# One block of a hybrid decoder: z by seven products of 256 columns, step widths as a block of their own, down's weight sums by a table

## The chip, the cores and the metric

The program runs on one core of a Trainium2 chip. The metric is the time of one execution on the device in microseconds; the kernel before has a median of 1806.73 us over three runs (1806.51 to 1807.75). A profile is one execution of the same program, recorded by the hardware: its own time was 1806.8 us and the recorded span 1804.9 us. The core has a matrix engine (TensorE, PE in the profile, its weight loads PEld), a vector engine (VectorE, DVE), a scalar engine (ScalarE, ACT), GpSimd (POOL) and SyncE (SP), which here issues nearly all transfers.

## What is computed

One layer on 1024 tokens of 1024 channels, in float32. Cut to what matters here:

```python
h = rms_norm(x, pre_norm1_w) * (1 + sc1) + sh1
z, xbc, dt_raw, q, k, v, gates = split(h @ w_in)   # z: 1024 columns, dt_raw: 16
# state-space branch, 16 heads in chunks of 128 tokens
xbc = silu(causal_conv(xbc) + conv_b)
dt = softplus(dt_raw + dt_bias)
a_cum = cumsum(dt * -exp(a_log))       # over the tokens of a chunk, per head
y = ssd_chunked(...)                   # decays exp(a_cum[t] - a_cum[s])
y = (y + d_skip * xs) * silu(z)
y = rms_norm_by_group(y, eps=1e-5) * ssd_norm_w
# attention branch from q, k, v; both branches are merged by sigmoid(gates)
x = x + g1 * rms_norm(mix, post_norm1_w)
h2 = rms_norm(x, pre_norm2_w) * (1 + sc2) + sh2
u = causal_conv(h2 @ w_up)
f = (gelu(u_gate) * u_val) @ w_down
x = x + g2 * rms_norm(f, post_norm2_w)
```

A product of float32 matrices is made of three matrix products on TensorE: each factor is split into a high part (rounded to the matrix engine's format) and a low part (the rest), and high × high, high × low and low × high are added up. The function `split` does that for weights: the high part is a copy on ScalarE (L95), the low part a subtraction on VectorE (L96).

## The kernel before, in words

The order of instructions on TensorE, VectorE, ScalarE and SyncE is the order in which the code is written: these parts stand in a manual schedule, and a few generators and tables say at which point of a stage a side task takes its next step. Each engine goes through its own row in order and waits where an instruction's input or buffer is not ready.

**Opening** (to 94.83 us). h is made and transposed; the first projections and the gates' blocks 0 to 3 are computed as 24 matmuls of 512 columns for each half of the tokens. While the last gate blocks run, VectorE and ScalarE form sums and differences of the four quarters of h (first or second half of the channels, first or second half of the tokens): the left factors `t1` to `t4`. `gate_split` (L270) splits a gate block's weights, `gate_half` (L515) issues its matmuls, `gate_out` (L350) puts the result through an activation and stores it.

**Pairs** (94.83 to 380.75 us). Fifteen pairs of 256 columns each (q, k, xbc and gates). In place of eight products of quarter blocks, seven products of sums are made; `order` lists them with the quarter or sum of h that each uses (`b11`, `b21`, `t2`, `t1`, `t3`, `b22`, `t4` for the weights; `HX` for h) and the bank of PSUM into which it adds. `x_sum` (L400) forms the weight sums on VectorE, `x_split` their high and low parts, `post` (L456) evacuates a pair while the next one runs (for the convolution: three steps on VectorE per block, L499). In the last five pairs a side task runs: `all_sums` (L547) forms, for the last matrix of the layer (down), four sums of weight blocks for each of 11 k, 44 in all, and stores them for later. Two sets of tiles `wdr` are used in turn; 16 sums are made before z.

**z** (380.75 to 473.57 us). z and the 16 columns of dt_raw are one product of 1040 columns, in three thirds of 346, 346 and 348: for each third and each of eight blocks of 128 tokens `mm3` (L117 to L119) issues 24 matmuls, with h as the stationary factor. Each result goes through tanh on ScalarE (L970) and one step on VectorE (L971) and is stored; the first 16 columns of the first third become dt (L966). Beside it run the remaining 28 sums for down, the last pair's evacuation, the weights of the next third, and the decays: `decays_a` (L852 to L883: softplus of dt by a series of small steps, then `la` = dt × −exp(a_log)), `decays_b` (cumulative sums by two small matmuls, L887) and `decays_c` (transposes of them, L900, copied and stored for the chunks).

**v and the chunks** (from 473.57 us). v's matmuls (`v_stream`, L1042 to L1053) run with the chunks of the state-space branch between them (`chunk_in`, `chunk_decay`, ...). For v, weights are split by `split_v` (L912).

## Time and profile before

| | |
|---|---|
| median of three runs | 1806.73 us (1806.51 to 1807.75) |
| the profiled execution, its span | 1806.8 us, 1804.9 us |
| granted clock of TensorE, mean | 0.998 |
| busy share of the span: TensorE, VectorE, ScalarE, GpSimd | 99%, 76%, 51%, 6% |
| end of the opening, pairs, z | 94.83, 380.75, 473.57 us |
| z: TensorE, VectorE, ScalarE busy | 92.82, 56.35, 25.89 of 92.82 us |

A row of the stage table gives the stretch, its length, then busy us and the number of instructions of PE, PEld, DVE, ACT and POOL, then the granted clock, the share of the transfer engines and GB/s. In a row of single instructions the first number is the start, the second the duration; what stands in square brackets is the idle time of the engine just ahead of it and what ended it. In a row of a group stand the shape, the count, busy us, the mean duration in ns, and the idle time ahead of the group's instructions with what ended most of it. TensorE's matmuls overlap, so the distance from start to start is what one costs.

### The profile page before, as it was taken

The numbers are of one execution on the slowest core, as the hardware profiler recorded it, in microseconds if no ns is written. First come the engines' busy times: TensorE is split into PE (matmuls) and PEld (weight loads), VectorE is DVE, ScalarE is ACT, GpSimd is POOL, SyncE is SP. The second block draws the span as 40 slices with busy tenths as digits, with TensorE's granted clock in tenths as the row PEclk, the third lists the DMA queues.
The fourth block names the chain that finished last, engine by engine and source line by source line (L and its number), as shares of the span: only waits on it lengthen the run. The fifth ranks groups of instructions, "written<-read, shape, count | busy, mean of one in ns | idle before, by whom it ended". The sixth has DMA issues, their size and how long they took to land.

```text
span 1804.9 us, 24533 instructions
## 1 busy us (share of the span) xinstructions
PE 1782.1 (99%) x8749; PEld 1494.7 (83%) x8749; DVE 1364.5 (76%) x2245; ACT 919.6 (51%) x1794; POOL 111.7 (6%) x110
## 2 busy tenths in 40 slices
PE   8999999999999999999999999999999999999998
PEld 6788888899977888888888888888888888888887
DVE  6896788976488777666667876689898888875555
ACT  4454444543457556665555443665554554554532
POOL 0000000000155400000000000100000000000001
PEclk9999999999999999999999999999999999999999
DMA  9565687678878886679842576413232223378754
GB/s 358 190 213 172 240 273 257 189 243 274 272 255 243 253 254 172 178 205 278 260 145 100 181 254 253 152 53 117 99 129 99 100 100 111 123 244 288 239 164 165
DMA packets 165322, 356.18 MB, mean 197 GB/s; under 512 B 16064, under 2 KB 64976, under 8 KB 165200
## 3 DMA queue, kind: packets, MB, share of 16 engines
q1 hardware_dynamic: 165200, 354.62, 60.2%
q8 instruction: 69, 1.13, 0.3%
q14 instruction: 53, 0.43, 0.1%
HBM read 248.83 MB, written 103.62 MB: 195 GB/s over the span
## 4 chain that ended last, share of the span: by engine, by line
PE 55%; DVE 6%; DMA 5%; ACT 3%; issue 1%; SPq 1%; POOL 0%; DVEq 0%; POOLq 0%; ACTq 0%
PE upx L2025 4%; PE upx L2026 4%; PE upx L2024 4%; PE o L1531 2%; PE upy L2025 2%; PE upy L2024 2%; PE upy L2026 2%; PE dx L2416 2%; PE dx L2417 2%; PE dx L2415 2%; PE mix L2085 1%; PE mix L2087 1%; PE mix L2086 1%; PE at L1518 1%; DMA gst<-gld_a 1%
## 5 line engine op out<-in xcount | busy, mean ns | idle before, releaser
L2024 PE MATMUL upx<-t,wu_t 128*128 128x512 f32 x264 | 103.1, 391 | 0.5 <-DVE cv L2480 0.4
L2025 PE MATMUL upx<-t,wu_t 128*128 128x512 f32 x264 | 102.8, 390 | 0.2 <-DVE t L2142 0.2
L2026 PE MATMUL upx<-t,wu_t 128*128 128x512 f32 x264 | 102.8, 389 | 0.0
L1456 DVE CUSTOM_DVE_ANT_0 sc<-sc,mw 128x256 f32<-128x256 f32 (+7 forms) x128 | 96.2, 772 | 8.5 <-PE sc L1469 7.2
L1998 ACT ACTIVATE wu_t<-sab 128x512 fp32r<-128x512 f32 x57 | 34.1, 627 | 127.7 <-DVE sab L2015 127.7
L1519 ACT COPY aT<-at 128x512 f32<-128x512 f32 (+2 forms) x96 | 46.0, 479 | 95.7 <-PE at L1518 95.4
L96 DVE TENSOR_TENSOR g_lo<-gst,g_hi 128x1024 fp32r<-128x1024 f32 (+1 forms) x42 | 47.4, 1135 | 49.5 <-ACT g_hi L95 49.5
L1531 PEld LDWEIGHTS o<-vt,aT 128*128 128x128 f32 x576 | 76.0, 191 | 6.0 <-ACT aT L1519 0.7
L1531 PE MATMUL o<-vt,aT 128*128 128x128 f32 x576 | 79.9, 275 | 0.2 <-ACT aT L1519 0.2
L397 ACT ACTIVATE xw_t<-xsab 128x512 fp32r<-128x512 f32 x45 | 27.3, 627 | 94.6 <-DVE xsab L406 94.6
L95 ACT ACTIVATE g_hi<-gst 128x1024 fp32r<-128x1024 f32 (+1 forms) x42 | 41.3, 988 | 65.3 <-DMA gst<-gld_s 39.1
L422 PE MATMUL xx<-xt,xw_t 128*128 128x512 f32 x180 | 70.2, 390 | 0.0
L423 PE MATMUL xx<-xt,xw_t 128*128 128x512 f32 x180 | 70.1, 389 | 0.0
L424 PE MATMUL xx<-xt,xw_t 128*128 128x512 f32 x180 | 70.0, 389 | 0.0
L1468 PE MATMUL sc<-kst,qst 128*128 128x512 f32 (+2 forms) x192 | 66.0, 352 | 0.0
L1506 DVE RECIPROCAL rsm<-ssum 128x2 f32<-128x2 f32 x64 | 10.6, 166 | 72.9 <-ACT p L1497 39.7
L1469 PE MATMUL sc<-klo,qst 128*128 128x512 f32 (+2 forms) x192 | 63.3, 346 | 0.3 <-DMA klo<-kld 0.3
L2042 DVE SCALAR_TENSOR_TENSOR ug<-cg,vec,ug 128x1023 f32<-128x1023 f32 (+1 forms) x44 | 56.3, 1280 | 6.1 <-ACT ug L2041 5.3
L2002 DVE TENSOR_TENSOR wu_t<-sab,wu_t 128x512 fp32r<-128x512 f32 x57 | 39.3, 690 | 26.6 <-ACT wu_t L1998 26.6
L2024 PEld LDWEIGHTS upx<-t,wu_t 128*128 128x128 f32 x264 | 49.5, 188 | 11.8 <-DVE cv L2480 1.4
L2025 PEld LDWEIGHTS upx<-t,wu_t 128*128 128x128 f32 x264 | 49.6, 188 | 10.7 <-DVE t L2142 0.5
L1510 DVE SCALAR_TENSOR_TENSOR p<-p,coef,p 128x512 f32<-128x512 f32 (+2 forms) x96 | 56.6, 617 | 2.3
(580 smaller groups left out, 5804.1 us busy)
## 6 DMA issues: line engine op xcount, KB each, us to landing
adas<-in_w_ada SPq DMA_DIRECT2D x32, 512.0 KB, 6.2
wdr<-in_w_down SPq DMA_DIRECT2D x22, 512.0 KB, 5.2
wtd<-wdr SPq DMA_DIRECT2D x22, 512.0 KB, 3.4
wuf<-in_w_up SPq DMA_DIRECT2D x22, 512.0 KB, 3.5
gld_s<-gsum SPq DMA_DIRECT2D x22, 512.0 KB, 2.8
gst<-gld_s SPq DMA_DIRECT2D x20, 512.0 KB, 5.1
wdt_raw<-wtd SPq DMA_DIRECT2D x20, 512.0 KB, 4.4
wuv<-in_w_up SPq DMA_DIRECT2D x19, 512.0 KB, 3.5
```

The source lines that it names most:

```text
L422: T.matmul(o, wh, xh_, start=(k == 0 and first), stop=False, skip_group_check=not first)
L423: T.matmul(o, wh, xl_, start=False, stop=False, skip_group_check=not first)
L424: T.matmul(o, wl, xh_, start=False, stop=(k == KH - 1), skip_group_check=not first)
L1456: V.tensor_tensor_reduce(out=sc, in0=sc, in1=mw[:, S - L :], scale=1.0, scalar=3.0e38, op0=ALU.add, op1=ALU.min, accum_out=col)
L1468: T.matmul(sc[:, n0:n1], qs_[s][:, tsl], ks_[s][:, n0:n1], start=True, stop=False)
L1469: T.matmul(sc[:, n0:n1], qs_[s][:, tsl], kl[s][:, n0:n1], start=False, stop=True)
L1510: V.scalar_tensor_tensor(pr[0][:, ksl], pr[1][:, ksl], coef[:, bq : bq + 1], pr[0][:, ksl], op0=ALU.mult, op1=ALU.add)
L1531: T.matmul(po_of[j, grp][:, qi, :], at[:, k, :], vt[j % 2][:, kt, :], start=(kt == 0), stop=(kt == i))
L2024: T.matmul(out_, wh, xh_, start=(k == 0 and first), stop=False, skip_group_check=not first)
L2025: T.matmul(out_, wh, xl_, start=False, stop=False, skip_group_check=not first)
L2026: T.matmul(out_, wl, xh_, start=False, stop=(k == end), skip_group_check=not first)
L2042: V.scalar_tensor_tensor(u[:, d:], c_[:, : S - d], fw[:, 2 - d : 3 - d], u[:, d:], op0=ALU.mult, op1=ALU.add)
```

## The change

z becomes a product of the same kind as the pairs. Its 1024 columns are two halves of 512; a column group g takes 256 columns of each half, and for each of two groups seven products are made of four blocks of 128 tokens and 12 matmuls of 256 columns each. `z_sum` makes weight sums on VectorE, `z_split` high and low parts, `z_mms` the matmuls, `z_keep` copies a result out of PSUM on ScalarE, `z_out` adds a kept one on VectorE and applies Silu on ScalarE, then stores. The tiles `t1` to `t4` of h live through z, and one quarter of h is loaded again at z's end. The factor one half that came with tanh goes (`nwr` is no longer scaled, the norm's divisor changes).

The 16 columns of dt_raw become a block in the opening: `wdt` is a tile of 128 columns per k, of which 16 hold the high and 16 the low parts and the rest zero (set by GpSimd). 32 matmuls of 512 columns use it as the stationary factor, two copies on ScalarE bring the result to `dtacc`, and eight small matmuls with `sel` turn it and add the parts; VectorE adds dt_bias.

The sums for down are placed by a table (`down_at`: s is a sum, l a load); one set of tiles is used in pairs 2 to 5 and from pair 9, and a second one in z. The decays' steps are placed by `run_decays`. The accumulated sums and their transposes use other PSUM banks. The loads of the first decays and of z's rows are issued elsewhere.

```diff
+    def z_sum(i, g):
+        a11, a12, a21, a22 = (zleft[n, g] for n in ("a11", "a12", "a21", "a22"))
+        o, x_, y_, op = ((a21, a21, a22, ALU.add), (a11, a21, a11, ALU.subtract), (a21, a22, a11, ALU.subtract), (a12, a12, a11, ALU.subtract))[i]
+        V.tensor_tensor(o, x_, y_, op=op)
+
+    def z_split(i):
+        g, p = divmod(i, 7)
+        n = order[p][0]
+        hi = wp.tile([P, KH, ZW], F32R, tag="whi", name=f"wz{g}{n}_hi", bufs=4)
+        lo = wp.tile([P, KH, ZW], F32R, tag="wlo", name=f"wz{g}{n}_lo", bufs=4)
+        split(hi, lo, zleft[("a11", "a12", "a11", "a21", "a21", "a12", "a22")[p], g])
+        zop[i] = hi, lo
...
-    def down_sums(k):
-        (b11, b12), (b21, b22) = [(t[:, 0, :], t[:, 1, :]) for t in wdr[k % 2]]
-        V.tensor_tensor(b11, b12, b11, op=ALU.subtract)
-        yield
...
+    def down_sum(k, i):
+        (b11, b12), (b21, b22) = [(t[:, 0, :], t[:, 1, :]) for t in wset(k)]
+        o, x_, y_ = ((b11, b12, b11), (b12, b22, b12), (b22, b22, b11), (b21, b21, b22))[i]
+        V.tensor_tensor(o, x_, y_, op=ALU.subtract)
+        if i % 2 == 1:
+            SP.dma_start(wtd[i // 2][:, k, :, :], wset(k)[i // 2])
...
+    down_at = {(2, 4): "l", (2, 5): "l", (3, 3): "s", (3, 5): "s", (4, 0): "s", (4, 1): "ls", (4, 3): "l", (4, 5): "s", (4, 6): "s", (5, 2): "s", (5, 4): "s"}
...
+        wdt = wp.tile([P, KD, P], F32R, tag="whi", name="wdt", bufs=4)
+        G.memset(wdt.bitcast(F32), 0.0)
+        SP.dma_start(wdt_raw.rearrange("p k c -> p (k c)"), a["w_dt"])
...
+        split(wdt[:, :, :NH], wdt[:, :, NH : 2 * NH], wdt_raw)
+        V.reduce_sum(sel, ident.rearrange("p (j n) -> p n j", n=NH), axis=AX.X)
...
         pg_ = gate_half(2, 1)
+        pdt = [ps_wb("dt0"), ps_wc("dt1")]
+        for half in range(2):
+            for k in range(KD):
+                for n in range(2):
+                    T.matmul(pdt[half], wdt[:, k, :], hT[k][half][:, n, :], start=(k + n == 0), stop=(k == KD - 1 and n == 1))
         gate_out(pg, 0, gsd[2], vev)
+        dtacc = wp.tile([P, 2, HALF], F32, tag="wlo", name="dtacc", bufs=4)
+        for half in range(2):
+            A.copy(dtacc[:, half, :], pdt[half])
         gate_split(3)
         x_load()
...
+        pd = ps_wb("dt")
+        for i in range(8):
+            T.matmul(pd[:, i * NH : (i + 1) * NH], dtacc[:, i // 4, i % 4 * P : (i % 4 + 1) * P], sel, start=True, stop=True)
+        V.tensor_tensor(dtr, pd[:, :P].rearrange("p (c h) -> p c h", h=NH), rows[:, None, R_DTB : R_DTB + NH].broadcast_to([P, 8, NH]), op=ALU.add)
...
-        pa = ps_wa("acum_ps")
+        pa = ps_wc("acum_ps")
...
-            pt = ps_wa(f"acT_ps{half}")
+            pt = (ps_wb, ps_wc)[half](f"acT_ps{half}")
...
+    def z_mms(g, p, qs=range(4)):
+        n, bk = order[p]
+        bk = "X" if bk == "X" else "Y"
+        first = p in (0, 1, 3)
+        if first:
+            z_banks(g, bk, p, qs)
+        wh, wl = zop[7 * g + p]
+        for q in qs:
+            o = zbank[g, bk, q]
+            tsl = slice(q * P, (q + 1) * P)
+            for k in range(KH):
+                xh_, xl_ = HX[n][k][:, 0, tsl], HX[n][k][:, 1, tsl]
+                T.matmul(o, xh_, wh[:, k, :], start=(k == 0 and first), stop=False, skip_group_check=not first)
+                T.matmul(o, xh_, wl[:, k, :], start=False, stop=False, skip_group_check=not first)
+                T.matmul(o, xl_, wh[:, k, :], start=False, stop=(k == KH - 1), skip_group_check=not first)
+
+    def z_keep(g, bk, e, qs=range(4)):
+        for q in qs:
+            A.copy(zev[e][:, q, :], zbank[g, bk, q])
+
+    def z_out(g, h, half, bk, e, o):
+        t = zout[o]
+        for q in range(4):
+            if e is None:
+                A.activation(t[:, q, :], zbank[g, bk, q], AF.Silu)
+            else:
+                V.tensor_tensor(t[:, q, :], zbank[g, bk, q], zev[e][:, q, :], op=ALU.add)
+        if e is not None:
+            A.activation(t, t, AF.Silu)
+        z0 = HALF * h + ZW * g
+        SP.dma_start(zdh[half][:, :, z0 : z0 + ZW], t)
...
-                mm3(ps, [((hT[k][half][:, 0, tsl], hT[k][half][:, 1, tsl]), (wz[k // 2][0][:, k % 2, :], wz[k // 2][1][:, k % 2, :])) for k in range(KD)])
...
-                A.activation(e[:, 0, :n], ps[:, lo:], AF.Tanh, scale=0.5)
-                V.scalar_tensor_tensor(e[:, 1, :n], e[:, 0, :n], 1.0, ps[:, lo:], op0=ALU.add, op1=ALU.mult)
-                SP.dma_start(zd[i][:, c0 + lo - NH : c0 + lo - NH + n], e[:, 1, :n])
...
+        z_mms(0, 0)
+        z_sum(1, 0)
+        z_split(2)
+        z_split(3)
+        z_keep(0, "X", 0)
+        posts(0)
+        z_mms(0, 1)
...
+        z_mms(0, 4)
+        z_out(0, 1, 1, "X", 0, 1)
+        z_split(7)
+        wdr.append([SL.get(f"wdr1{j}", F32, (P, 2, HALF)) for j in range(2)])
+        down("ssll")
+        run_decays(5)
...
+        z_mms(1, 1)
+        z_out(1, 0, 0, "Y", 0, 0)
+        run_decays(5)
+        z_sum(2, 1)
+        z_split(11)
+        v_raw.append(fetch_v(0, 1))
+        down("ll")
+        z_mms(1, 2)
+        z_keep(1, "X", 1)
+        assert next(dec, None) is None
+        decays_b()
+        z_split(12)
+        SL.put(*HX["t2"])
+        down("ss")
+        v_raw.append(fetch_v(0, 2))
+        z_mms(1, 3, (0, 1))
+        decays_c()
+        z_mms(1, 4, (0, 1))
+        z_keep(1, "Y", 0, (0, 1))
+        z_mms(1, 3, (2, 3))
+        z_keep(1, "Y", 0, (2, 3))
+        z_split(13)
+        v_raw.append(fetch_v(0, 3))
+        SL.put(*HX["t1"])
+        xch = [SL.get(f"xch{i}", F32, (P, KD, P)) for i in range(2)]
+        zown = [SL.get(f"zown{n}", F32R, (P, 2, HALF)) for n in range(2)]
+        M = [SL.get(f"M{n}", F32, (P, NH // 2, P)) for n in range(3)]
+        SP.dma_start(xch[0], xcd[:, 0])
+        down("ss")
+        z_mms(1, 4, (2, 3))
+        z_out(1, 1, 1, "X", 0, 1)
+        split_v(0, 0, v_raw.pop(0), zown)
+        down("ssll")
+        SL.put(*HX["t3"])
+        for n in range(3):
+            load_decay(n)
+        SP.dma_start(xch[1], xcd[:, 1])
+        z_mms(1, 5)
+        z_out(1, 0, 1, "Y", 1, 0)
+        split_v(0, 1, v_raw.pop(0))
+        split_v(0, 2, v_raw.pop(0))
+        down("ss")
+        new_b12((0, 1))
+        z_mms(1, 6)
+        z_out(1, 1, 0, "X", None, 1)
+        split_v(0, 3, v_raw.pop(0))
+        down("ssss")
+        new_b12((2, 3))
...
-            lambda: rstd_of(ssy[:, c, :], ssy[:, c, :], 1.0 / (4 * GW), 1e-5),
+            lambda: rstd_of(ssy[:, c, :], ssy[:, c, :], 1.0 / GW, 1e-5),
```

Three places of the instruction rows. First, ScalarE in the opening. `gs_0` and `gs_1` are results of gate blocks, `vev` their tiles, `wgs_hi` the high part of gate block 3's weights, `xt` parts of `t1` and `t3`, `dt` the block's result in PSUM. Before:

```order
L352 ACTIVATE vev_696<-gs_1_418 128x512 [waits PE_49]
L521 ACTIVATE xt_0_739<-hr_123 128x512
L521 ACTIVATE xt_1_740<-hr_123 128x512
L352 ACTIVATE vev<-gs_0_700 128x512 [waits DMAHW4_49,PE_49,Activation_49]
L95 ACTIVATE wgs_hi<-wgs_raw 128x1024 [waits DMAHW6_49]
L521 ACTIVATE xt_2_741<-hr_124 128x512
```

There the high part of the weights follows the gate block's activation. In the change:

```order
L352 ACTIVATE vev_695<-gs_1_414 128x512 [waits PE_49]
L95 ACTIVATE wdt<-wdt_raw 128x8x16 [waits DMAHW1_49,Pool_49]
L528 ACTIVATE xt_0_738<-hr_123 128x512
L528 ACTIVATE xt_1_739<-hr_123 128x512
L352 ACTIVATE vev<-gs_0_699 128x512 [waits DMAHW4_49,PE_49,Activation_49]
L735 COPY dtacc<-dt_778 128x512 [waits PE_49]
L735 COPY dtacc<-dt_779 128x512 [waits PE_49]
L95 ACTIVATE wgs_hi<-wgs_raw 128x1024 [waits DMAHW6_49]
```

Two copies of the new block's results and the high part of its weights stand ahead of `wgs_hi`; both copies wait for TensorE.

Second, VectorE around the decays' last steps (`sm1` holds the decays' small tiles, `la` and `acum` among them, `acum_ps` and `acT_ps` are PSUM tiles of the cumulative sums and of their transposes, `wdr` the tiles of down's sums). Before, with z's rows of the third matmul group between them:

```order
L882 SCALAR_TENSOR_TENSOR sm1_3039<-sm1_3039,aexp_3044 128x128 [waits DVE_49,Activation_49]
L535 TENSOR_TENSOR wdr10_2395<-wdr11_2396,wdr10_2395 128x512 [waits DMAHW7_49]
L971 SCALAR_TENSOR_TENSOR ev0_3041<-ev0_3041,z346_4_3496 128x346 [waits DMAHW4_49,Activation_49]
L540 TENSOR_TENSOR wdr11_2396<-wdr11_2396,wdr10_2395 128x512 [waits DMAHW3_49,DVE_49]
L542 TENSOR_TENSOR wdr11_2396<-wdr11_2396 128x512 [waits DVE_49]
L96 TENSOR_TENSOR wz692_0_lo_3554<-wz692_0_raw_3400,wz692_0_hi_3553 128x696 [waits DMAHW0_49,Activation_49]
L971 SCALAR_TENSOR_TENSOR ev1_3042<-ev1_3042,z346_5_3528 128x346 [waits DMAHW7_49,Activation_49]
L533 TENSOR_TENSOR wdr00_2274<-wdr00_2274 128x512 [waits DMAHW6_49,DMAHW1_49]
L971 SCALAR_TENSOR_TENSOR ev2_3043<-ev2_3043,z346_6_3561 128x346 [waits DMAHW2_49,Activation_49]
L889 COPY sm1_3039<-acum_ps_3589 128x128 [waits PE_49]
L892 TENSOR_TENSOR sm1_3039<-acum_ps_3589,sm1_3039 128x128 [waits DVE_49,Activation_49]
```

The copy of the cumulative sums (L889) comes eight rows behind `la` (L882). In the change, from the step that makes `la` (L907) on:

```order
L907 SCALAR_TENSOR_TENSOR sm1_3096<-sm1_3096,aexp_3098 128x128 [waits DVE_49]
L368 TENSOR_TENSOR wza211_3305<-zxr_3033,wza111_3303 128x1024
L96 TENSOR_TENSOR wz1t3_lo_3712<-wza211_3305,wz1t3_hi_3711 128x1024 [waits Activation_49]
L914 COPY sm1_3096<-acum_ps_3771 128x128 [waits PE_49]
L917 TENSOR_TENSOR sm1_3096<-acum_ps_3771,sm1_3096 128x128 [waits DVE_49,Activation_49]
L96 TENSOR_TENSOR wz1b22_lo_3780<-wza121_3367,wz1b22_hi_3779 128x1024 [waits Activation_49]
L543 TENSOR_TENSOR wdr00_2341<-wdr00_2341 128x512 [waits DMAHW4_49,DMAHW2_49]
L543 TENSOR_TENSOR wdr00_2341<-wdr01_2342,wdr00_2341 128x512 [waits DMAHW3_49,DVE_49]
L926 COPY acs_3814<-acT_ps0_3815 16x512 [waits PE_49]
L926 COPY acs_3814<-acT_ps1_3821 16x512 [waits PE_49]
```

A weight sum and a low part of z now stand between `la` and the copy of the cumulative sums, and a low part and two sums for down between that copy and the copies of the transposes.

Third, TensorE at the same place, in the change (`z10`, `z13` are PSUM tiles of z's second column group):

```order
L995 MATMUL z10_3_3582<-wz1t2_hi_3567,xt2_3_642 128x256
L912 MATMUL acum_ps_3771<-sm1_3096,tri_148 128x128 [waits DMAHW6_49,DVE_49]
L913 MATMUL acum_ps_3771<-sm1_3096,ones_87 128x128
L993 MATMUL z13_0_3788<-wz1t1_hi_3635,xt1_0_738 128x256 [waits Activation_49]
L994 MATMUL z13_0_3788<-wz1t1_lo_3636,xt1_0_738 128x256
...
L995 MATMUL z13_1_3789<-wz1t1_hi_3635,xt1_3_741 128x256
L925 MATMUL acT_ps0_3815<-ident_83,sm1_3096 16x128 [waits DVE_49]
L925 MATMUL acT_ps0_3815<-ident_83,sm1_3096 16x128 x3
L925 MATMUL acT_ps1_3821<-ident_83,sm1_3096 16x128 [waits DVE_49]
L925 MATMUL acT_ps1_3821<-ident_83,sm1_3096 16x128 x3
L993 MATMUL z10_0_3579<-wz1t3_hi_3711,xt3_0_742 128x256 [waits Activation_49]
```

The cumulative sums stand between product (1, 2) and product (1, 3), the transposes after the first half of (1, 3).

254 lines of the change are left out of this document (121 added, 133 removed).

## The prediction

> **What bounds the kernel now.** I first read the busy times of the whole span, then the table of busy time by stage, cut at the places where the program's stages change, and then single instructions at the cuts.
>
> ```profile
> PE 1782.1 (99%) x8749; PEld 1494.7 (83%) x8749; DVE 1364.5 (76%) x2245; ACT 919.6 (51%) x1794; POOL 111.7 (6%) x110
> ...
> core 0: us, PE busy (x) PEld busy (x) DVE busy (x) ACT busy (x) POOL busy (x), PEclk, DMA share, GB/s
> ...
> 73.00:94.83 21.83, 21.83 (x98) 18.02 (x96) 17.10 (x28) 14.26 (x26) 0.00 (x0) 1.00 0.33 114
> 94.83:380.75 285.92, 285.92 (x1262) 236.31 (x1260) 240.27 (x343) 134.03 (x209) 0.00 (x0) 1.00 0.68 227
> 380.75:473.57 92.82, 92.82 (x590) 92.44 (x589) 56.35 (x108) 25.89 (x46) 0.00 (x0) 1.00 0.84 281
> ```
>
> ```profile
> 94.60 0.39 PE L119 MATMUL gs<-hT,wgs_lo 128*128 128x512 f32 x1
> 94.83 0.39 PE L422 MATMUL xx<-hT,xw_b 128*128 128x512 f32 x1
> ...
> 380.75 0.32 PE L117 MATMUL z<-wz_hi,hT 128*128 128x346 f32 x1
> 380.90 0.32 PE L118 MATMUL z<-wz_lo,hT 128*128 128x346 f32 x1
> ...
> 473.57 0.60 PE L1123 MATMUL px<-ident,xch 128*128 128x128 f32 x4
> ```
>
> Three stages are touched: the end of the opening (to 94.83), the 15 pairs (to 380.75) and z (to 473.57). In all three TensorE is busy for the whole stretch at full clock, so it alone sets the time: fewer matmul microseconds shorten the kernel, and any wait that the change makes TensorE take lengthens it. The row of z has a second message: VectorE is busy for 56 of 93 us and ScalarE for 26, so today neither is near its limit.
>
> **z itself.** It falls from 576 matmuls of 346 columns to 2 × 7 × 4 × 12 = 672 of 256. One 512-column matmul in the pairs takes 285.92 / 1262 = 0.2266 us, one of z 92.82 us less about 1.1 us of fourteen small ones, over 576: 0.159 us. The trace has 256-column matmuls, each with its own weights:
>
> ```profile
> 705.00 0.28 PE L1468 MATMUL sc<-kst,qst 128*128 128x256 f32 x1
> 705.12 0.28 PE L1469 MATMUL sc<-klo,qst 128*128 128x256 f32 x1
> 705.24 0.40 PE L1468 MATMUL sc<-kst,qst 128*128 128x512 f32 x1
> ...
> 705.00 0.19 PEld L1469 LDWEIGHTS sc<-klo,qst 128*128 128x128 f32 x1
> 705.12 0.19 PEld L1468 LDWEIGHTS sc<-kst,qst 128*128 128x128 f32 x1
> ```
>
> Starts are 0.12 us apart; a straight line through 0.2266 and 0.159 gives 0.123, plain proportion to columns 0.117. I take 0.119: 672 × 0.119 = 80.0 us (bounds 78.6 and 82.7), with the small ones 81.1 against 92.8, so **−11.7 us** if nothing waits.
>
> **The step widths** are a new block of 32 matmuls of 512 columns: 32 × 0.2266 = +7.3 us. Eight small ones follow; sixteen matmuls of that kind take
>
> ```profile
> 484.06 2.02 PE L1165 MATMUL py<-xd,M 128*128 128x64 f32 x16
> ```
>
> 0.126 us each, so eight are +1.0. The block is where TensorE has no gap, hence all of it is on the path.
>
> **A wait behind the block.** After it TensorE starts gate block 3, whose first matmul needs ScalarE's high part of the weights and whose third needs VectorE's low part. Today:
>
> ```profile
> 79.66 0.64 ACT L352 ACTIVATE vev<-gs 128x512 f32<-128x512 f32 x1
> 80.14 1.11 ACT L95 ACTIVATE wgs_hi<-wgs_raw 128x1024 fp32r<-128x1024 f32 x1
> ...
> 81.28 1.22 DVE L96 TENSOR_TENSOR wgs_lo<-wgs_raw,wgs_hi 128x1024 fp32r<-128x1024 f32 x1 [0.66 <-ACT wgs_hi L95]
> ...
> L1519 ACT COPY aT<-at 128x512 f32<-128x512 f32 x48 | 28.2, 587 | 76.4 <-PE at L1518 76.4
> ```
>
> In the new order the two copies of the block's sums out of PSUM stand ahead of that high part on ScalarE, and the second can start only when TensorE has ended the block. So at the block's end: copy 0.59 + high part 1.06, TensorE waits 1.65; two matmuls later (0.45) the low part, which takes 1.22, is still 0.77 short. Sum **+2.4 us**, bounds 0 (the high part after all gets done before) and 2.9 (VectorE busy with the line before it). Queued behind the copies on ScalarE are also the parts of x that VectorE finishes for the pairs; VectorE then waits for the small matmuls before it makes the first x weights. It has about 6.9 us of work there and TensorE 24 + 12 matmuls of 0.2266 = 8.2 us, so that is covered, by 1.0 us. Opening: 7.3 + 1.0 + 2.4 = +10.7.
>
> **What feeds z.** Each of the 14 products now needs weights of its own (a high part on ScalarE, a low part on VectorE, for most a sum ahead of them), and its results are copied, added and put through Silu. VectorE's work in z stays in one row of instructions with the convolution, the decays and the sums for down. Their prices:
>
> ```profile
> L96 DVE TENSOR_TENSOR g_lo<-gst,g_hi 128x1024 fp32r<-128x1024 f32 x35 | 42.8, 1224 | 47.0 <-ACT g_hi L95 47.0
> L2046 DVE TENSOR_TENSOR ug<-ug,uv 128x1024 f32<-128x1024 f32 x22 | 26.8, 1219 | 0.1
> L499 DVE SCALAR_TENSOR_TENSOR xbcT<-xcv,vec,xbcT 128x1022 f32<-128x1022 f32 x6 | 7.7, 1282 | 0.0
> L249 DVE TENSOR_TENSOR wf_lo<-wf_raw,wf_hi 128x256 fp32r<-128x256 f32 x8 | 2.9, 420 | 0.0
> L542 DVE TENSOR_TENSOR wdr<-wdr 128x512 f32<-128x512 f32 x8 | 5.5, 687 | 0.0
> L872 DVE TENSOR_TENSOR sm<-sm,sm 128x128 f32<-128x128 f32 x6 | 1.8, 292 | 0.2
> L874 DVE TENSOR_SCALAR sm<-sm 128x128 f32<-128x128 f32 x6 | 1.4, 225 | 0.1
> L862 DVE RECIPROCAL sm<-sm 128x128 f32<-128x128 f32 x1 | 1.0, 953 | 0.0
> L901 DVE COPY acs<-acT_ps 16x512 f32<-16x512 f32 x2 | 1.3, 670 | 0.0
> L501 ACT ACTIVATE xbcT<-xbcT 128x1024 f32<-128x1024 f32 x3 | 3.2, 1057 | 3.7 <-DVE xbcT L499 3.7
> L858 ACT ACT_TABLE_LOAD x1 | 1.3, 1283 | 0.0
> L890 ACT ACTIVATE sm<-sm 128x128 f32<-128x128 f32 x1 | 0.3, 311 | 0.8 <-DVE sm L889 0.8
> L900 PE MATMUL acT_ps<-ident,sm 128*16 128x128 f32 x8 | 1.0, 272 | 0.0
> ```
>
> I followed VectorE's row from the end of product 2 (TensorE at 2 × 5.71 = 11.4 us into z; a product is 48 × 0.119) to the decays' last step, which writes `la`. In between: 7 low parts 8.5, 5 weight sums 6.1, 5 convolution steps 6.4, 13 additions 5.5, 8 sums for down 5.5, 21 decay steps about 6.0, ada's small ones 0.7: 38.7, some 0.7 less where starts overlap, so 38.0. To this come stretches in which VectorE must wait for ScalarE, because the low part next in its row needs a high part that itself is ordered behind a Silu that needed VectorE's last addition: Silu 1.06 and high part 1.06 two times in full and once half covered (5.4), the high part alone twice (2.2), an exponential and odd pieces 1.8: 9.4. A table load of 1.28 comes with each change between exponential and Silu, mostly under VectorE's work. So `la` is there at 11.4 + 38.0 + 9.4 = 58.8, and TensorE asks for it after ten products, at 57.1. That is the first wait, **1.7 us** (bounds 0 and 2.8). Second: the transposes of the sums stand after half a product more (61.9), but the copy that they read stands in VectorE's row behind a weight sum, a high part and a low part: 58.8 + 1.2 + 1.1 + 1.2 + 0.3 = 62.6, **0.7 us**. Third: after the transposes (1.0) and half of product 12, at 62.6 + 1.0 + 2.9 = 66.5, half of product 11 writes into the two PSUM banks of those transposes. They are emptied behind another low part, itself behind a table load, three exponentials and a high part on ScalarE, and behind two sums for down: 62.9 + 0.9 + 1.1 + 1.2 + 1.4 + 0.7 = 68.2, **1.7 us**. Together **+4.1 us**, with bounds 0 (the covers hold) and 8 (each of the three 1.3 longer, by one table load). z as a whole: −11.7 + 4.1 = −7.6.
>
> **The rest.** At the start of v TensorE waits today:
>
> ```profile
> 476.49 0.50 PE L1052 MATMUL v<-wv_lo,hT 128*128 128x512 f32 x1 [0.37 <-DVE wv_lo L920]
> ...
> 133.00:152.00 19.00, 14.72 (x21) 1.00 0.56 168
> ...
> 342.40:361.50 19.10, 17.12 (x23) 1.00 0.57 181
> ```
>
> The change makes all of the first v weights ready before z's end: −0.5 us with the row around it (bounds −0.5 and 0). The other rows are VectorE alone in pair 2 and in a late pair (busy us, then clock, DMA share and GB/s): 14.7 and 17.1 of 19. Of down's 44 sums 24 instead of 16 now come before z: eight in pairs 2 to 5, where at most four fall into one pair (4 × 0.69 = 2.8 us beside 14.7 or less in the second row), and still 16 in the late pairs, up to four where three stood (17.8 of 19.1). They use one pair of tiles instead of two, so that a sum can wait for its load, and VectorE's row behind it. I take 0 (bounds 0 and 1.3, what a late pair has left). The factor of the tanh that is dropped and the loads of the decays and of z's rows that move come off other engines than TensorE: 0.
>
> **Sum.** The profiled execution took 1806.8 us, as long as the median of the runs, 1806.73. 1806.8 + 10.7 − 7.6 − 0.5 = **1809.4 us**.
>
> **The rivals.**
>
> *Only the opening waits.* If VectorE is five microseconds faster along its row than I count (starts of long operations overlap, the ScalarE waits are shorter), z has no wait: 1809.4 − 4.1 = 1805.3. For it: `la` is late by only 1.7 of 58.8 us, and the third wait comes from the same delay. Against it: the order of the banks' copies behind a low part does not depend on the sum.
>
> *Nothing waits.* The opening's high part too is out of the way: 1805.3 − 2.4 = 1802.9. Against it: ScalarE's order is fixed, and the second copy can't start earlier than the block's end.
>
> *A wait trips the clock.* This ends on the slow side. The trace has what a wait can do after itself:
>
> ```profile
> 12.00:14.00 2.00, 0.07 (x1) 0.07 (x1) 0.75 (x7) 0.52 (x2) 1.02 (x1) 1.00 1.07 376
> 14.00:16.00 2.00, 2.00 (x14) 2.00 (x15) 2.00 (x4) 0.92 (x3) 0.00 (x0) 0.78 1.04 406
> 16.00:22.00 6.00, 5.23 (x14) 3.97 (x14) 5.09 (x12) 4.15 (x8) 0.00 (x0) 0.50 1.02 409
> ...
> 13.94 2.86 PE L213 MATMUL xtr<-diag,xt 128*128 128x128 f32 x16 [2.24 <-DMA wf_raw<-in_w_gate]
> ```
>
> An idle stretch of 2.24 us stands ahead of 2 us at 0.78 and 6 us at 0.50 of the clock. A busy TensorE loses 2 × 0.22 + 6 × 0.50 = 3.4 us in such a stretch. If one of the waits that I predict (1.65 and 0.77 close together, or 1.7) does the same, the time is 1809.4 + 3.4 = 1812.8; it decides from an idle stretch of somewhere under 2.24 us. Against it: there TensorE had idled more than once before, here it comes from hundreds of busy microseconds. [...]
>
> *The weights bind.* Loads of weights take 0.19 us each in the rows at 705. If they ran one after another, 672 of them would take 127 us, z would last 35 us longer than today with all else covered, and the time would be 1806.8 + 10.7 + 35 − 0.5 = 1852. Against it: the rows at 705 start 0.12 us apart, so two loads overlap, and z itself has loads of that length every 0.159 us. But only two such matmuls in a row are shown.
>
> **How the numbers follow.** My forecast (opening late, `la` and the banks late) has 0.43; with its own bounds, 1807 to 1813. Only the opening 0.25, nothing 0.12, the clock 0.15, the weights 0.02, other 0.03. The likeliest is 1809.4. The range 1801.5 to 1815.5 takes in the second and third cases and the clock's, with 2 in 10 left out for longer waits, the pairs' VectorE and weight loads. A difference under 0.2% (3.6 us) can't be told from none here, so faster means under 1803.1 and slower over 1810.3: faster 0.19 (most of the third case, the fast end of the second), slower 0.37 (the clock, the weights, 0.4 of the first), the same 0.44.
>
> **What would show it.** In the changed profile: z 85 us long and 256-column matmuls 0.119 apart (wrong if 0.123 or more, or if PEld sets the pace); TensorE idle before the first matmul of gate block 3 with ScalarE's `wgs_hi` named (1.65), and before the third with VectorE's `wgs_lo` (0.77); idle before the sums of the decays with VectorE named (1.7), before the transposes (0.7) and in product 11 (1.7); granted clock 1.00 behind each. No idle in z would show the VectorE sum wrong; idle in the pairs would show that the moved sums for down cost something; a clock under 1.00 in either place is the third rival.

## The result, and the profile after

The changed kernel takes 1824.57 us (median of four runs, 1823.13 to 1827.77) against 1806.62 us. The ratio of the means is 1.0106, with a 95% interval of 1.0085 to 1.0126. The forecast was 1809.4 us in a range of 1801.5 to 1815.5. It is 1% slower, seven times what was forecast (18.0 us against 2.6).

The table of busy time by stage for the changed kernel (stretch, length, busy us and instructions of PE, PEld, DVE, ACT, POOL, then granted clock, transfer share, GB/s), cut at the start of the step widths' block, the pairs, the first matmul of z and the first of v:

```profile
core 0: us, PE busy (x) PEld busy (x) DVE busy (x) ACT busy (x) POOL busy (x), PEclk, DMA share, GB/s
81.43:104.18 22.75, 20.59 (x97) 16.67 (x96) 10.44 (x17) 7.35 (x13) 0.00 (x0) 1.00 0.10 35
104.18:392.88 288.70, 285.26 (x1249) 233.79 (x1248) 243.51 (x350) 133.00 (x208) 0.00 (x0) 1.00 0.69 234
392.88:488.24 95.36, 87.84 (x699) 85.70 (x698) 62.75 (x100) 42.59 (x66) 0.00 (x0) 0.98 0.53 181
```

Before, TensorE was busy for the whole of each stage. Now it is idle in all three: 2.2, 3.4 and 7.5 us. (The last product of the last pair, 12 matmuls or 2.72 us, now stands behind the first seven matmuls of z, so the pairs end 2.72 us later than the cut shows.) The rows of TensorE that had to wait for an input, with the wait and what ended it in brackets:

```profile
90.47 0.50 PE L117 MATMUL gs<-hT,wgs_hi 128*128 128x512 f32 x1 [1.63 <-ACT wgs_hi L95]
91.73 0.50 PE L119 MATMUL gs<-hT,wgs_lo 128*128 128x512 f32 x1 [0.53 <-DVE wgs_lo L96]
110.73 0.50 PE L427 MATMUL xx<-xt,xw_t 128*128 128x512 f32 x1 [0.95 <-ACT xevs L805]
238.95 0.50 PE L427 MATMUL xx<-xt,xw_t 128*128 128x512 f32 x1 [1.73 <-DVE xcv L819]
...
393.74 0.39 PE L994 MATMUL z<-wz0b_lo,hT 128*128 128x256 f32 x1 [0.58 <-DVE wz0b_lo L96]
400.59 0.39 PE L993 MATMUL z<-wz0b_hi,hT 128*128 128x256 f32 x1 [2.53 <-DVE xcg L823]
460.98 0.49 PE L912 MATMUL acum_ps<-sm,tri 128*128 128x128 f32 x2 [2.17 <-DVE sm L907]
466.40 0.60 PE L925 MATMUL acT_ps<-ident,sm 128*16 128x128 f32 x4 [1.12 <-DVE sm L917]
470.87 0.39 PE L993 MATMUL z<-wz1t_hi,xt 128*128 128x256 f32 x1 [1.00 <-DVE acs L926]
521.34 1.10 PE L1298 MATMUL pst<-xdd,sm 128*128 128x512 f32 x2 [1.17 <-DVE xd L1255]
524.44 0.66 PE L1247 MATMUL px<-ident,xch 128*128 128x128 f32 x4 [1.29 <-DVE tt L1281]
529.72 1.13 PE L1280 MATMUL pq<-prev,xbcT 128*128 128x512 f32 x2 [1.53 <-DVE prev L1300]
```

Five of them stand where the prediction put them (the two ahead of gate block 3 at 90.47 and 91.73, the three of the decays at 460.98, 466.40 and 470.87). The others were not forecast. Behind two groups of them the clock fell (TensorE alone: stretch, length, busy us and instructions, clock, transfer share, GB/s):

```profile
398.06:400.59 2.53, 0.00 (x1) 1.00 0.00 2
...
402.00:405.00 3.00, 3.00 (x16) 0.50 0.02 5
...
532.00:538.00 6.00, 6.00 (x18) 0.50 1.04 384
```

In slices of 1.5 us, the time lost to the lower clock adds up to 1.7 us behind the wait at 400.59 and 3.4 us behind the one at 529.72.

By stage (before, after), in us: to the first matmul of the pairs 94.83, 104.18 (+9.35); the pairs 285.92, 291.42 (+5.50); z to the first matmul of v 93.51, 92.64 (−0.87); the rest 1330.64, 1334.66 (+4.02). Together +18.0, the difference of the two spans. In the first of these the changed kernel was 2.5 us ahead before any of its new work began: the wait for h at the last convolution weights stands at 69.51 instead of 71.99. This is the execution and not the change: the profile before had run at half clock around 16 to 22 us (a row of the prediction), that of the changed kernel has a clock of 1.00 from 14 to 22 us. So the new work of the opening costs 9.35 + 2.48 = 11.8.

### The profile page after: what moved, and what is told of

It is laid out like the page before. It is cut to its first block, busy times and chain, and to the rows that moved or that the text cites. A ratio compares the mean times of both kernels' runs of the same rounds, so it can differ in the third digit from the quotient of the medians.

```text
span 1822.9 us, 24778 instructions
## 1 busy us (share of the span) xinstructions
PE 1786.5 (98%) x8893; PEld 1494.7 (82%) x8893; DVE 1375.5 (75%) x2249; ACT 935.8 (51%) x1817; POOL 111.7 (6%) x111
## 4 chain that ended last, share of the span: by engine, by line
PE 76%; DVE 11%; DMA 5%; ACT 5%; issue 2%; SPq 0%; POOL 0%; DVEq 0%; POOLq 0%; ACTq 0%
PE upx L2141 4%; PE upx L2140 4%; PE upx L2142 4%; PE o L1647 3%; PE xx L427 2%; PE xx L428 2%; PE xx L429 2%; PE upy L2141 2%; PE upy L2140 2%; PE upy L2142 2%; PE dx L2532 2%; PE dx L2533 2%; PE dx L2531 2%; PE dy L2531 2%; PE dy L2533 2%
## 5 line engine op out<-in xcount | busy, mean ns | idle before, releaser
L2140 PEld LDWEIGHTS upx<-t,wu_t 128*128 128x128 f32 x264 | 49.6, 188 | 11.7 <-DVE cv L2596 1.4
```

The lines of the kernel that those rows point to most:

```text
L2140: T.matmul(out_, wh, xh_, start=(k == 0 and first), stop=False, skip_group_check=not first)
```

## The experiments

The kernels e1 to e3, e5 and e7 each make one move in the changed kernel, e4 two that belong together, e8 to e10 several. Beside the medians the stages of their profiles tell more, since a move shows in one stage. "Opening" runs from the step widths' block to the pairs, "z" from its first matmul to v's less the 2.72 us of the pair, and "clock" is the time lost to a lower clock in each of the stages, as above.

| | median us | ratio to before | opening | pairs | z | rest | clock: opening, pairs, z, rest |
|---|---|---|---|---|---|---|---|
| before | 1806.62 | | | 285.92 | 93.51 | 1330.64 | 0, 0, 0, 0 |
| changed | 1824.57 | 1.0106 | 22.75 | 291.42 | 92.64 | 1334.66 | 0, 0, 1.7, 3.4 |
| e1 loads first | 1822.01 | 1.0088 | 24.29 | 291.14 | 89.71 | 1332.31 | 1.7, 0, 1.7, 0 |
| e2 store early | 1821.62 | 1.0083 | 22.75 | 289.09 | 91.49 | 1331.78 | 0, 0, 0, 0 |
| e3 split first | 1820.12 | 1.0077 | 19.98 | 292.08 | 92.50 | 1332.16 | 0, 0, 3.4, 0 |
| e4 decays early | 1829.93 | 1.0126 | 24.34 | 293.40 | 95.60 | 1334.32 | 1.7, 1.7, 3.4, 0 |
| e5 b12 later | 1826.46 | 1.0122 | 24.30 | 292.25 | 92.44 | 1332.75 | 1.7, 0, 3.4, 0 |
| e7 Silu later | 1820.06 | 1.0087 | 22.76 | 291.67 | 89.68 | 1331.94 | 0, 0, 1.7, 0 |
| e8 mended | 1811.53 | 1.0039 | 19.98 | 288.77 | 86.66 | 1329.94 | 0, 0, 0, 0 |
| e9 with b12 | 1810.32 | 1.0034 | 19.97 | 288.82 | 86.22 | 1331.72 | 0, 0, 0, 0 |
| e10 more | 1806.78 | 1.0011 | 19.98 | 288.18 | 83.72 | 1329.70 | 0, 0, 0, 0 |

The kernel before ran beside each set, with medians of 1806.83 (e1 to e4), 1804.66 (e5 to e9) and 1805.20 (e10); the ratios are to the mean of those. From one set to another the same kernel differs by up to 2 us, so across sets the ratio says more than the difference of two medians.

A loss to the clock can't simply be subtracted from a stage. The profiles of e1, e3 and e5, in which the clock fell to 0.50 behind the decays' first wait, have no wait ahead of the transposes, where the changed kernel, at 1.00, waits 1.12 us: there the slower TensorE likely came to the transposes only when VectorE was done. Stages are best compared between profiles that lost the same at the same place.

### e1: z's loads ahead of a store

The wait of 2.53 us is for the evacuation of a PSUM bank by VectorE (L823), but VectorE itself had been held. Its row and SyncE's at that place in the changed kernel (for SyncE: start, time to issue, the transfer):

```profile
383.66 0.43 SPq L362 DMA_DIRECT2D wza<-in_w_z  x1
389.46 0.34 SPq L545 DMA_DIRECT2D wtd<-wdr  x1
389.85 1.30 SPq L362 DMA_DIRECT2D wza<-in_w_z  x2
391.19 0.69 SPq L362 DMA_DIRECT2D zxr<-in_w_z  x1
```

```profile
388.75 0.69 DVE L543 TENSOR_TENSOR wdr<-wdr 128x512 f32<-128x512 f32 x1
389.35 0.69 DVE L403 TENSOR_TENSOR xw_t<-xwv,xw_t 128x512 fp32r<-128x512 f32 x1
...
397.57 1.23 DVE L368 TENSOR_TENSOR wza<-wza,zxr 128x1024 f32<-128x1024 f32 x1 [2.09 <-DMA zxr<-in_w_z]
398.71 1.22 DVE L96 TENSOR_TENSOR wz0b_lo<-wza,wz0b_hi 128x1024 fp32r<-128x1024 f32 x1
399.85 0.69 DVE L823 TENSOR_TENSOR xcg<-xy,xevs 128x512 f32<-128x512 f32 x1
```

The store of a sum for down stands ahead of three of z's four loads, and SyncE can issue it only when VectorE has made the sum (388.75 + 0.69): the loads leave 6 us behind the first one. z's first weight sum waits for the last of them, and the evacuation stands behind that sum.

```diff
+            if (k, i) == (5, 3):
+                held.append(lambda: SP.dma_start(wtd[1][:, 5, :, :], wset(5)[1]))
...
                     for n in {1: ("a11",), 2: ("a21",), 3: ("a12", "a22")}.get(p, ()):
                         z_load(n, 0)
+                    if p == 3:
+                        held.pop()()
```

> One edit of the changed kernel: the store of down's 24th sum is issued on SyncE behind z's first four weight loads instead of ahead of three of them; nothing else moves. Theory (a store that waits for a sum holds the loads of z back): the weights of a22 land about 5 us earlier, VectorE's 2.09 us wait for them goes, TensorE's wait of 2.53 us behind the first 12 matmuls of z goes, and with it the stretch at half clock (402.0 to 405.2): 2.5 + 0.2 + 1.6 = 4.3 us less than the changed kernel, about 1820.3. The 0.58 us wait for the first low part stays. Rival (VectorE has too much work there): the loads land early, but TensorE still waits 1.5 us or more for VectorE in the first 4 us of z, and the time falls by under 1 us.

1822.01 us (1820.66 to 1824.09), 2.6 less, with runs that overlap those of the changed kernel (1823.13 to 1827.77). The wait fell from 2.53 to 1.07 us and there was no lower clock behind it. So the store was about 1.5 us of the wait. The rest has two more causes. In e1 two of the four loads still leave over 6 us behind the first: e1's rows of SyncE, what SyncE waited for there (us in all, times, longest), and the row of VectorE's sum:

```profile
387.55 6.78 SPq L362 DMA_DIRECT2D wza<-in_w_z  x3
394.37 0.51 SPq L362 DMA_DIRECT2D zxr<-in_w_z  x1
...
SPq L362 <- DVE xw_t L403: 5.3, 1, 5.3
...
400.00 1.22 DVE L368 TENSOR_TENSOR wza<-wza,zxr 128x1024 f32<-128x1024 f32 x1 [0.64 <-DMA zxr<-in_w_z]
```

The third load goes into the space of the pairs' last weights, and SyncE waits until VectorE has read them (L403). In the changed kernel that read ends at 390.04 and the load leaves at 390.3, so the store held mainly the second load back. And the evacuation still stands behind the sum: in e8, where TensorE's wait is 1.42, the sum waits 0.98 us for its load; in e10, where the sum stands behind the evacuation, TensorE's wait is gone. Whether that move alone would have been enough was not run.

The saving in the median is less than the 4.3 expected. In e1's profile the opening and the decays' wait each cost 1.7 us of clock that they had not cost before, but the other three executions had a clock of 0.998 to 1.000, so this does not explain the median.

### e2: a store ahead of four loads

In pair 6 VectorE waits 6.14 us to write a tile whose space was that of a sum for down (SyncE's row, then VectorE's, in the changed kernel):

```profile
216.40 1.76 SPq L446 DMA_DIRECT2D adas<-in_w_ada  x4
218.26 0.99 SPq L545 DMA_DIRECT2D wtd<-wdr  x1
```

```profile
215.18 0.69 DVE L543 TENSOR_TENSOR wdr<-wdr 128x512 f32<-128x512 f32 x1
...
227.92 1.23 DVE L495 SCALAR_TENSOR_TENSOR xql<-xcg,xqh 128x1024 fp32r<-128x1024 f32 x1 [6.14 <-DMA wtd<-wdr]
```

The sum is done at 215.9, its store leaves at 218.3 behind four loads of 512 KB, and has landed only at 227.9.

```diff
-    down_at = {(2, 4): "l", (2, 5): "l", (3, 3): "s", (3, 5): "s", (4, 0): "s", (4, 1): "ls", (4, 3): "l", (4, 5): "s", (4, 6): "s", (5, 2): "s", (5, 4): "s"}
+    down_at = {(2, 4): "l", (2, 5): "l", (3, 3): "s", (3, 5): "s", (4, 0): "s", (4, 1): "ls", (4, 3): "l", (4, 5): "s", (4, 6): "s", (5, 2): "s", (5, 3): "s"}
```

> One edit of the changed kernel: down's 8th sum is made after product 3 of pair 5 instead of product 4, so that its store is issued ahead of four loads of 512 KB and not behind them. Theory (the tile of that sum is given to the next user before its store has landed): VectorE's wait of 6.14 us for the store in pair 6 goes, TensorE's wait of 1.73 us and the 0.3 us ones in pairs 5 and 6 go: 2.4 us less, about 1822.2. Rival (the eight sums as VectorE's work): the same eight sums cost the same, pairs 5 and 6 stay at 19.47 and 21.40 us, no change.

1821.62 us (1819.54 to 1822.32), 3.0 less; the pairs fell by 2.33 us to 289.09, and the wait of 1.73 us is gone. The same eight sums are still made, so this part was not VectorE's amount of work.

### e3: gate block 3's weights first

```diff
+        gate_split(3)
         dtacc = wp.tile([P, 2, HALF], F32, tag="wlo", name="dtacc", bufs=4)
         for half in range(2):
             A.copy(dtacc[:, half, :], pdt[half])
-        gate_split(3)
```

> One edit of the changed kernel: ScalarE makes the high part of gate block 3's weights ahead of the two copies of the step widths' sums. Theory: TensorE's waits of 1.63 and 0.53 us ahead of gate block 3 go, with 0.2 us of restart: 2.4 us less, about 1822.2. Rival (the wait only moves, since ScalarE is late with all that follows): the wait of 0.95 us in pair 0 for ScalarE's copy grows to 2 to 3 us, and the time falls by under 1 us.

1820.12 us (1819.62 to 1821.03), 4.5 less. The opening fell from 22.75 to 19.98 us, both waits are gone, and the wait in pair 0 stayed at 0.95. ScalarE's order alone made them, as the prediction had it. More than the 2.4 us expected was saved; in the profiles the remainder stands in the rest of the program, which lost 3.4 us to the clock in the changed kernel and none here.

### e4: the decays earlier

```diff
         down("ss")
+        run_decays(5)
         z_mms(0, 4)
...
-        run_decays(5)
-        z_sum(2, 1)
-        z_split(11)
         v_raw.append(fetch_v(0, 1))
...
         decays_b()
-        z_split(12)
+        z_sum(2, 1)
+        z_split(11)
...
-        down("ss")
...
         decays_c()
+        z_split(12)
+        down("ss")
```

> One edit of the changed kernel: the decays' steps begin one product earlier in z, and the weight sum and parts of products 12 and 13 are made behind the copies of the cumulative sums and of their transposes instead of ahead. Theory (order on VectorE, not its amount): the waits of 2.17, 1.12 and 1.00 us are down to 0.5 us together, 3.8 us less, about 1820.8. Rival (VectorE and ScalarE together are too slow for z): the waits come back at the products whose weights are now made later, together 3 us or more, and the time falls by under 1 us.

1829.93 us (1827.07 to 1831.94), 5.4 more: my theory fell. z takes 95.60 us, 3.1 more than in e3 and e5, which change nothing in z and lost the same 3.4 us there. Rows of TensorE's waits in e4:

```profile
447.12 0.36 PE L993 MATMUL z<-wz1b_hi,hT 128*128 128x256 f32 x1 [1.35 <-DVE zout L1007]
465.42 0.49 PE L912 MATMUL acum_ps<-sm,tri 128*128 128x128 f32 x2 [0.80 <-DVE zout L1007]
...
471.98 0.45 PE L993 MATMUL z<-wz1t_hi,xt 128*128 128x256 f32 x1 [1.61 <-ACT wz1t_hi L95]
473.23 0.58 PE L994 MATMUL z<-wz1t_lo,xt 128*128 128x256 f32 x1 [0.81 <-DVE wz1t_lo L96]
```

What was taken ahead pushed the additions back, whose PSUM banks TensorE then needed, and the parts made later were late. The rival that VectorE and ScalarE together are too slow for z had it right for this order; but which of their work, or only their order, was open, since VectorE is busy for 63 of the 92 to 98 us from z's start to v's in the changed kernel and in e1 to e4.

### e7: Silu behind the next high part

VectorE's additions, ScalarE's Silu of them, ScalarE's high part for the next product and VectorE's low part made one chain, though the high part needs nothing of the Silu. In e7 `z_out` issues the additions only and returns a function for Silu and store; one of six places:

```diff
-        z_out(0, 1, 1, "X", 0, 1)
-        z_split(7)
+        end = z_out(0, 1, 1, "X", 0, 1)
+        z_split(7)
+        end()
...
```

> One edit of the changed kernel: ScalarE makes the high part of the next product's weights ahead of the Silu of the result just added, at six places in z; VectorE's and TensorE's rows stay. Theory (VectorE is not short of time in z, it waits for ScalarE, whose Silu waits for VectorE's additions): four such places lie ahead of the decays' last step, each 1.06 us shorter, so the wait of 2.17 us is gone and 1.12 and 1.00 fall to 1 us together: 3.2 us less than the changed kernel, about 1821.3. Rival (the sum of VectorE's own work sets it): the waits for the decays stay over 3 us together, under 1 us less.

1820.06 us (1819.86 to 1821.02), 4.5 less; by the ratios, which allow for the faster set, 3.4 less. The first of the three waits is gone, the second is 0.67, the third still 1.00: 4.29 us became 1.67, a little less than hoped. z fell from 92.64 to 89.68 us, with the same clock loss at the same place. No instruction was taken away. So the larger part of these waits, 2.6 of 4.3 us, came not from VectorE's amount of work but from the two engines waiting for each other in turn.

### e5 and e9: four loads later

```diff
     def new_b12(ks):
         for k in ks:
             hT[k][1] = new_hl(f"b12_{k}")
-            SP.dma_start(hT[k][1].rearrange("p h t -> p (h t)").bitcast(F32), h12d[k])
...
+            if u == 0:
+                load_b12()
```

> One edit of the changed kernel: the four loads of h's last quarter (512 KB each), needed by v's fifth token block, are issued behind the first loads for the attention output instead of at z's end. Theory (the transfers of z's end fill the transfer engines and hold the chunks' loads back): VectorE's wait of 6.38 us for those loads is under 3 us, TensorE's waits of 1.17, 1.29 and 1.53 us in the first chunks fall to 1 us together, 3.0 us less than the changed kernel, about 1821.5. Rival (too much is in transit anyway, or SyncE is held by the load of z's rows that waits for z's stores): the waits stay and the time falls by under 1 us.

1826.46 us (1826.08 to 1826.64), no gain. VectorE's wait for the loads of the attention output fell only from 6.38 to 4.50 us, and others of 0.85 and 2.44 came; TensorE's waits in the first chunks moved and did not shrink (0.82, 1.88 and 1.69, together 4.4 us instead of 4.0). My theory on the four loads fell. SyncE had been held ahead of the load of z's rows, 5.2 us in the changed kernel and 2.5 here, as the rival says; the profile names the landing of the last of down's sums, issued behind z's stores, as the end of that wait, and it does not show whether z's own stores held it too. The rest of the program, 1332.75 us, is close to the 1331.8 to 1332.3 us of e1 to e3, which had no lower clock there either, so most of the 4.0 us that the changed kernel lost here is likely the 3.4 us of clock. It is not certain: e4, without a lower clock there, has 1334.32.

> e8 with the edit of e5 as well. Theory: 3 us less than e8, about 1809. Rival: as e8 within 1 us.

1810.32 us (1808.04 to 1811.56) against 1811.53 for e8: 1.2 less, within the spread of both, and the rest of the program got no shorter (1331.72 against 1329.94). That is nearer to the rival (within 1 us) than to the theory (3 us).

### e8: the moves together

e1, e2, e3 and e7, with VectorE's addition of dt_bias, which waits for TensorE's eight small matmuls, behind the first weights of the pairs:

```diff
-        V.tensor_tensor(dtr, pd[:, :P].rearrange("p (c h) -> p c h", h=NH), rows[:, None, R_DTB : R_DTB + NH].broadcast_to([P, 8, NH]), op=ALU.add)
         x_split(0, 0)
...
         x_split(0, 2)
+        V.tensor_tensor(dtr, pd[:, :P].rearrange("p (c h) -> p c h", h=NH), rows[:, None, R_DTB : R_DTB + NH].broadcast_to([P, 8, NH]), op=ALU.add)
         pg_ = gate_half(3, 1)
```

> The changed kernel with the edits of e1, e2, e3 and e7, and with VectorE's addition of dt_bias behind the first weights of the pairs instead of ahead. Theory (the lost time is made of separate waits, each with its own place in a row of instructions, which add up): opening 2.8, pair 0 1.2, pairs 5 and 6 2.3, z's beginning 2.9, z's decays 3.2 less: 12.4 us less than the changed kernel, about 1812. Rival (what is taken away at one place is lost at the next): under 8 us less, 1817 or more.

1811.53 us (1809.72 to 1813.12): 13.0 less than the changed kernel, by the ratios 12.1, where 12.4 were expected. The total is near, and partly by luck. The opening gave 2.8 us as expected. The pairs gave 2.65 of 3.5, since pair 0's wait only went from 0.95 to 0.61. z is 86.66 us against 91.49 in e2, which has z's orders unchanged and also lost no clock there: 4.8 of 6.1. In the profile the clock made up for it: the changed kernel lost 3.4 us to it in the rest of the program, which the expectation had not counted, and e8 none. So the waits did not move on to the next place, as the rival had it, but the three stages alone give 10.2 us.

The wait in pair 0 is ended by ScalarE's copy of a PSUM bank. ScalarE's rows in the changed kernel:

```profile
106.52 2.68 ACT L528 ACTIVATE xt<-hr 128x512 fp32r<-128x512 f32 x4 [1.35 <-DVE hr L289]
...
110.10 0.58 ACT L805 COPY xevs<-xx 128x512 f32<-128x512 f32 x1
```

The copy stands behind high parts that had waited for VectorE, and VectorE's row there begins with the addition that waits for the small matmuls.

### e10: four more

```diff
-                    elif p == 5:
+                    elif p == 6:
                         z_sum(0, 0)
                         z_split(1)
...
         decays_c()
+        z_split(12)
+        down("ss")
...
-    down_at |= {(11, 6): "ls", (12, 1): "l", (12, 3): "s", (12, 4): "s", (12, 6): "s", (13, 0): "ls", (13, 2): "l", (13, 4): "s", (13, 5): "s"}
+    down_at |= {(11, 6): "ls", (12, 1): "l", (12, 3): "s", (12, 5): "s", (12, 6): "s", (13, 0): "ls", (13, 2): "l", (13, 5): "s", (13, 6): "s"}
...
             ao_step(*ao_end.get(u, ((), ())))
+            if u == 0:
+                load_z(0)
```

> e8 with four more moves: z's first weight sum and second split behind the evacuation of the last pair's bank; the copies of the decays' transposes ahead of product 13's weight parts and two sums for down; one sum for down in pairs 12 and 13 behind the evacuation there instead of ahead; the load of z's rows behind the first loads for the attention output. Theory (each of e8's waits has its own place and they add up): pairs 1.2 less, z's beginning 1.5, z's decays 1.1, chunks 1.5, together 5.3 us less than e8 (1811.5), about 1806, which is level with the kernel before to within 0.2%. Rival (the rest of e8's excess is work on TensorE, 9.1 us for the step widths against 11.7 saved, and the waits move on to the next place): 1809 or more.

1806.78 us (12 runs, 1804.62 to 1812.17) against 1805.20, a ratio of 1.0011 with an interval of 1.0001 to 1.0021: level with the kernel before to within 0.2%, but not below it. Against e8 z gave 2.9 us (2.6 expected), the pairs 0.6 of 1.2 (the waits of 0.30 us in pairs 12 and 13 are gone, so there the sum for down had stood in front of an evacuation), the rest of the program 0.2 of 1.5. Its stages:

```profile
82.12:102.10 19.98, 19.98 (x97) 16.80 (x96) 9.64 (x16) 6.95 (x13) 0.00 (x0) 1.00 0.11 39
102.10:387.56 285.46, 284.65 (x1250) 233.72 (x1248) 243.45 (x350) 132.85 (x207) 0.00 (x0) 1.00 0.69 238
387.56:474.00 86.44, 85.18 (x698) 84.01 (x697) 65.28 (x103) 43.52 (x68) 0.00 (x0) 1.00 0.59 202
```

z is 83.72 us against 93.51 before, 9.8 less. What is left takes that back: the step widths, which cost

```profile
81.43 7.42 PE L731 MATMUL dt<-hT,wdt 128*128 128x512 f32 x32
...
96.90 1.85 PE L752 MATMUL dt<-sel,dtacc 128*128 128x16 f32 x16
```

9.1 us in all (rows of the changed kernel, 19.98 less 48 matmuls of gate block 3 at 0.2266), and 2.3 us in the pairs, of which the wait in pair 0 (0.61) and its restart (1.00 and 0.33 us between starts instead of 0.227) are 0.9; most of the rest lies at five places where two matmuls each start 0.34 to 0.53 us after the one before instead of 0.227. No version was found that beats the kernel before.

## Why the prediction was wrong, by its own steps

**What bounds the kernel: right.** TensorE sets the time: what the change lost over its forecast lies mostly where TensorE waited, restarted or ran at half clock, and taking waits away (e8, e10) gave the time back.

**z's matmuls: right, slightly low.** A product takes 5.76 to 5.83 us, so 0.120 to 0.121 a matmul where 0.119 was taken: 0.8 us more over 672. Weight loads, 0.19 us each, did not bind: with one for each matmul the starts stayed 0.12 us apart.

**The step widths: block right, small ones mis-sized.** 32 × 0.2266 = 7.25 as forecast; the eight small matmuls take 1.85 us instead of 1.0. Here a row was misread: the profile lists these eight matmuls of the program as 16, and the row at 484.06, from which the price was taken (16 in 2.02 us), is also a loop of eight (L1165). Eight of that kind take 2.0 us, not 1.0.

**The wait behind the block: right.** 1.63 and 0.53 measured, 1.65 and 0.77 forecast, and e3 shows ScalarE's order as the cause. The cover that was named for VectorE's next work (1.0 us in the text, 8.2 − 6.9 = 1.3 by its own figures) was not there: pair 0 waits 0.95 us, for a copy of ScalarE that is late because VectorE is. VectorE's first x weights stood behind an addition that waits for the small matmuls, and these came later and were longer than in the sum; moving that addition (e8) gave back a third of it.

**What feeds z: place and size right, cause half right.** The three waits were forecast as 1.7, 0.7 and 1.7 us and measured as 2.17, 1.12 and 1.00: 4.29 in place of 4.1. The near total is partly luck, since the third was 0.7 too high and the first two 0.9 too low. But e7 shows that most of it hung on one order on ScalarE. The 9.4 us of waits for ScalarE in the working were taken as given there; they were the term that could be moved.

**"The rest" is the step that failed.** It set the moved sums for down at 0 in the pairs because VectorE has time for them. The pairs took 5.5 us more. VectorE has the time; e2 shows that 2.3 us of the loss come from a store behind four loads, on whose landing the next user of the tile waits. About 1.2 us are pair 0's wait of 0.95 and its restart (1.33 and 0.34 us between starts instead of 0.227), and two waits of 0.30 us stand where a sum was put ahead of an evacuation (e10). And for z's beginning the prediction followed VectorE's row only from product 2 on and never SyncE's, and so put nothing there; two waits, 0.58 and 2.53 us, and 1.7 us of clock behind them followed. A sum moved into pair 14 brings its store, and the store stood ahead of three of z's four loads (1.5 us of the wait by e1); the other part is the space of the last loads and VectorE's order. The working counted a moved sum's 0.69 us and left out its transfer.

**The start of v: right, and outweighed.** Its wait of 0.37 us is gone, but the chunks behind it lost more: the rest of the program is 4.0 us longer, with 3.4 us lost to the clock. In e2, without such a loss, it is 1.1 us longer.

**The clock: a rival with too low a chance and too few places.** It was given 0.15 and 3.4 us, behind the forecast waits. In the profiled execution it cost 1.7 us in z and 3.4 us in the chunks, both behind waits that were not forecast; behind forecast ones it fell in e1, e3, e4 and e5. In seven profiles of kernels with long waits left in (the changed one, e1 to e5, e7) it cost 0 to 6.8 us from the opening's new block on. The profiled execution was no exception: the four executions of the changed kernel had mean clocks of 0.995 to 0.997, which is by the means, as an estimate, 5 to 9 us lost in each, while seven of the kernel before (beside e1 to e4) had 0.998 to 1.000.

In the sum: opening +11.8 in place of +10.7, pairs +5.5 in place of 0, z −0.9 in place of −7.6, the rest +4.0 in place of −0.5, less 2.5 us by which that profile was ahead at the start. Those 2.5 us are luck of the execution; without them the miss would have been larger.

## What to carry to other kernels

Where a step is moved in a kernel with orders written out, follow its transfers on the issuing queue as well as its instructions: here a store that waited for a late result held the loads behind it (one load of z left 6 us later), a load waited until the old contents of its space had been read (5.3 us in e1), and a tile handed on was free only when its store had landed (VectorE waited 6.1 us for one in pair 6). Where two engines feed each other in turn, take out of the chain what nothing in it needs (2.6 us of waits in e7), before moving work between stages. A saving on the engine that sets the time is worth its full amount only if none of the engines that feed it is asked in an order that makes it wait; here 9.1 us of new matmuls took back most of a saving forecast at 11.7, and waits of 0.3 to 2.5 us each, with the clock behind some of them, did the rest. And compare the number of instructions in a row of the profile with the calls in the code before taking a price from it.
